# Bias-table copies in DRAM: the outermost dimension of the copies changed from the pair of heads (4) to query column and head (32)

## The chip, the cores and the metric

The kernel runs on one core of one Trainium2 chip. The metric is device time in microseconds (us). Three runs before the change took 1340.88, 1342.46 and 1348.09 us; the median is 1342.46 us.

## The reference, cut to what matters

One encoder layer over 2048 tokens of width 1024: an input projection, then two branches side by side (neighbourhood attention of 8 heads on a 32 x 64 grid, and a bidirectional mLSTM of 4 heads), an output projection, a gated residual and a last RMSNorm. What the change touches is the additive bias of the attention:

```python
dy = row_idx - r[:, None] + NA_KH - 1
dx = jnp.clip(col[None, :] - col[:, None], -(NA_KW - 1), NA_KW - 1) + NA_KW - 1
bias = rpb[:, dy[:, None, :, None], dx[None, :, None, :]]
s = jnp.einsum('bhrcd,bhrjkd->bhrcjk', qg, kg).astype(jnp.float32) + bias[None]
s = jnp.where(col_mask[:, None, :], s, -jnp.inf)
```

`rpb` has 8 heads x 15 row offsets x 31 column offsets. The kernel works on patches of 8 x 16 queries, and for each kind of patch (3 kinds of rows x 3 kinds of columns) it needs a table with the negated bias of every query against every key of the patch's window, and 1e30 where the window does not reach.

The layer's other work that the change lies beside: a centred convolution of width 5 with a SiLU over the mLSTM's q and k, the transposes of k, and the output weight multiplied by the gate.

## The kernel before, in words

**Stages.** (1) `start` normalises the tokens and computes the first two v/o blocks of the projection. (2) `tok_blocks` computes blocks 2 to 5, with tokens on partitions: v and o of two mLSTM heads (tiles `pvo`, stored through `stvo`) and the attention's v (tiles `pv`, stored through `stv`), 128x256 matmuls, 16 tiles a block. Beside them run the mLSTM's decay tables: `decays` loads a row of `d_mneg` into one of six tiles `dec` (line 822, on the SP queue), GpSimd masks it (826), ScalarE takes four exponentials (833), and the ACT queue stores it to `d_ck` (835); 32 such tiles. (3) `conv_blocks` computes blocks 6 to 9 with channels on partitions: 32 tiles `pc` of 24 matmuls of 128x512 each (lines 546 to 548). ScalarE evicts each into a tile `u` (line 891, 4 buffers), VectorE makes the convolution `acc` of five operations (926 and 928, 5 buffers), ScalarE applies SiLU (930), SP stores it (933). For k, TensorE then transposes it (`kt`, line 939, four transposes), ScalarE copies that into one of two stage tiles `stk` (941), and SP stores it (943). In the same stage `gated_out` loads the output weight in 16 halves `wraw` (854, two buffers), VectorE multiplies each by the gate (861), SP stores it to `d_wo` (862). (4) `phase1b` and `phase2` do the mLSTM, the rest of the projection (tiles `pq`, line 986) and the attention; the tables are loaded there into `tab` (1450).

**The bias tables.** They are made in DRAM alone, by copies on the SP queue. `tables_begin` writes the negated `rpb` to `d_rneg` and fills the column tables `d_e` with 1e30; `tables_columns` then copies for each of the 16 query columns of a kind the 16 column offsets that it sees: 3 kinds x 16 = 48 copies `d_e<-d_rneg` of 4 x 30 x 16 floats (line 648). `tables_rows` copies for each kind of columns, kind of rows and query row 8 rows of the column table into `d_t`: 3 x 3 x 8 = 72 copies `d_t<-d_e` (line 670) of 4 x 32 pieces, each of 8 x 24 or 8 x 32 floats (768 or 1024 bytes). In both, the outermost 4 is the pair of heads, and the next dimension is the query column and the head of the pair (2), or the head of the pair and the row offset.

**Order of the work.** Stages (2) and (3) are ordered by a scheduler that places each engine's instructions by its own estimate of their costs, DMAs included. Each queue then runs strictly in that order: an instruction that waits holds up all that stand behind it on its engine. The scheduler also gives the DMAs of the SP and ACT queues eight completion semaphores in turn, so that a DMA waits, before its issue, for the landing of the one that used its semaphore last. The stage (4) is ordered by hand.

Of the kernel before, what the change touches and what calls it, by code (L numbers as in the profile page):

```python
# [62 lines left out]
class Kernel:  # L63
# [576 lines left out]
    def tables_columns(self, ct):  # L640
        nc = self.nc
        c0 = (0, 16, 48)[ct]
        k0 = (0, 8, 40)[ct]
        for i in range(16):
            c = c0 + i
            start = min(max(c - 8, 0), GRID_W - 16)
            dx = start - c + 15
            nc.sync.dma_start(self.d_e[ct][:, i, :, :, start - k0 : start - k0 + 16].rearrange("h e a k -> h (e a) k"), self.d_rneg.rearrange("(h e) a k -> h (e a) k", e=2)[:, :, dx : dx + 16])

    def table_fills(self):  # L650
        nc = self.nc
# [8 lines left out]
    def tables_rows(self, ct, rt):  # L660
        nc = self.nc
        nk = (24, 32, 24)[ct]
        pr = (0, 1, 3)[rt]
        t = self.d_t[rt][ct]
        for r in range(8):
            row = 8 * pr + r
            start = min(max(row - 4, 0), ROWS - 8)
            dy = start - row + 7
            j0 = (start - PR_R0[pr]) * nk
            nc.sync.dma_start(  # L670
                t[:, r * 16 : (r + 1) * 16, :, j0 : j0 + 8 * nk].rearrange("h q e n -> h (q e) n"),
                self.d_e[ct][:, :, :, dy : dy + 8, :].rearrange("h c e a k -> h (c e) (a k)"),
            )


# [1140 lines left out]
```

## Time and profile before

| what | value |
|---|---|
| three runs, us | 1340.88, 1342.46, 1348.09 |
| the profiled execution, us | 1339.01 |
| its span, us (1.81 us lie around it) | 1337.2 |
| mean granted TensorE clock | 0.992 |
| TensorE matmul busy | 1296.3 us, 97% |
| VectorE busy | 780.4 us, 58% |
| ScalarE busy | 541.6 us, 41% |
| GpSimd busy | 224.6 us, 17% |
| DMA | 255.89 MB, 228645 packets, mean 191 GB/s |
| `d_t<-d_e` on SP, line 670 | 72 issues, 281.6 to 484.2 us |
| `d_e<-d_rneg` on SP, line 648 | 48 issues, 143.2 to 280.5 us |

In a row of the profile, PE is TensorE's matmul, PEld its weight load, DVE VectorE, ACT ScalarE, POOL GpSimd and SPq the SP queue, which issues DMAs. Times are us from the span's start unless a row says ns; three numbers with slashes are the least, the median and the greatest of a group, in ns. PEclk is the share of full clock that TensorE was granted. The DMA share is the mean over the core's 16 DMA engines of the time in which they had packets; packets that wait in an engine's queue can take it over 1. Matmuls overlap in TensorE, so that a busy share of 97% is no measure of what is left; the idle time and the clock are.

### The profile page before, as it was taken

To read this page: it belongs to the slowest core of one execution; us is meant where nothing else is said; L and a number is where in the kernel's file an instruction comes from. 1 tells how busy PE (TensorE), PEld (TensorE's weight loads), DVE (VectorE), ACT (ScalarE), POOL (GpSimd) and SP (SyncE) were. 2 spreads that over 40 slices of the span, in tenths; PEclk is the share of its full clock that TensorE was granted. 3 is DMA by queue.
4 is the path that set the end of the run, shared out by engine and by line. 5 is a ranking of instruction groups with operands and counts; after the bars stand their busy time and mean duration, and the time that the engine had idled before them with its cause. 6 is when DMAs were issued, how large, how long until landed. Compare 5 with 4: busy or idle time off the path is not lost.

```text
span 1337.2 us, 23272 instructions
## 1 busy us (share of the span) xinstructions
PE 1296.3 (97%) x8330; PEld 1116.4 (83%) x8330; DVE 780.4 (58%) x2406; ACT 541.6 (41%) x1184; POOL 224.6 (17%) x278
## 2 busy tenths in 40 slices
PE   9999999999999879999999999999998999999996
PEld 8899999999888667888888888888776777778785
DVE  5645442112552929456677877777647676766663
ACT  5653325542212403223333423333346555565551
POOL 0243103441000000001212102212102211212211
PEclk9999999999999999999999999999999999999999
DMA  9997547896364856644665867755678876767771
GB/s 324 331 268 186 160 136 185 220 232 182 107 160 125 199 139 187 194 119 138 190 181 177 248 200 207 224 174 172 199 251 234 217 206 184 193 179 192 201 185 48
DMA packets 228645, 255.89 MB, mean 191 GB/s; under 512 B 29734, under 2 KB 177958, under 8 KB 228530
## 3 DMA queue, kind: packets, MB, share of 16 engines
q1 hardware_dynamic: 145326, 182.97, 48.2%
q0 software_dynamic: 20464, 36.21, 10.9%
q10 hardware_dynamic: 62740, 35.22, 9.1%
q8 instruction: 66, 1.08, 0.3%
q14 instruction: 49, 0.40, 0.1%
HBM read 169.81 MB, written 92.72 MB: 196 GB/s over the span
## 4 chain that ended last, share of the span: by engine, by line
PE 64%; DMA 14%; issue 7%; DVE 6%; SPq 5%; ACT 2%; POOL 1%; ACTq 0%; POOLq 0%; DVEq 0%
PE pq L986 20%; PE y L1566 12%; SPq L670 4%; PE pvo L546 3%; PE pO L1521 3%; PE pvo L548 3%; PE pvo L547 3%; PE pvo L601 3%; PE pT L1506 3%; DMA d_ck<-dec 3%; PE pS L1478 2%; DMA tab<-d_t 2%; DMA dec<-d_mneg 2%; PE pi L1227 2%; PE px L1225 2%
## 5 line engine op out<-in xcount | busy, mean ns | idle before, releaser
L986 PE MATMUL pq<-hhi,whi_a 128*128 128x512 f32 x512 | 208.4, 407 | 2.0 <-ACT u L891 2.0
L986 PE MATMUL pq<-hlo,whi_a 128*128 128x512 f32 x512 | 208.1, 406 | 0.0
L986 PE MATMUL pq<-hhi,wlo_a 128*128 128x512 f32 x512 | 206.7, 404 | 0.0
L986 PEld LDWEIGHTS pq<-hhi,whi_a 128*128 128x128 f32 x512 | 96.8, 189 | 18.7 <-ACT u L891 2.5
L986 PEld LDWEIGHTS pq<-hhi,wlo_a 128*128 128x128 f32 x512 | 96.8, 189 | 16.6
L986 PEld LDWEIGHTS pq<-hlo,whi_a 128*128 128x128 f32 x512 | 96.8, 189 | 16.1 <-issue 0.5
L1508 ACT ACTIVATE pt<-pT 96x384 f32<-96x384 f32 (+3 forms) x128 | 65.7, 514 | 84.0 <-PE pT L1506 81.1
L960 POOL TENSOR_TENSOR wlo_a<-rawq,whi_a 128x1024 fp32r<-128x1024 f32 x19 | 45.8, 2411 | 316.2 <-ACT whi_a L959 282.0
L1487 ACT ACTIVATE pbuf<-pbuf,mn 128x480 f32<-128x480 f32 (+5 forms) x128 | 76.0, 595 | 50.7 <-DVE mn L1486 50.6
L1566 PE MATMUL y<-hhi,whi_a 128*128 128x512 f32 x256 | 90.7, 416 | 0.5 <-ACT whi_a L1536 0.5
L1566 PE MATMUL y<-hhi,wlo_a 128*128 128x512 f32 (+1 forms) x272 | 90.6, 399 | 0.2 <-ACT y L1573 0.2
L1230 ACT ACTIVATE num<-px,gtile 128x129 f32<-128x129 f32 x120 | 38.2, 365 | 112.8 <-PE px L1225 90.7
L1486 DVE CUSTOM_DVE_ANT_0 pbuf<-pS,tab 128x480 f32<-128x480 f32 (+5 forms) x128 | 62.4, 539 | 36.7 <-PE pS L1478 29.0
L618 DVE TENSOR_TENSOR stvo<-pvo,brow 128x256 f32<-128x256 f32 x64 | 26.6, 423 | 83.7 <-PE pvo L548 64.6
L1506 PEld LDWEIGHTS pT<-ident,pbuf 128*128 128x128 f32 (+2 forms) x416 | 50.6, 136 | 27.0 <-issue 6.9
L546 PE MATMUL pvo<-whi_b,hhi 128*128 128x256 f32 x256 | 72.6, 284 | 0.0
L1506 PE MATMUL pT<-ident,pbuf 128*128 128x128 f32 (+2 forms) x416 | 66.8, 273 | 5.9 <-DVE pbuf L1498 4.3
L548 PE MATMUL pvo<-whi_b,hlo 128*128 128x256 f32 x256 | 72.0, 281 | 0.0
L547 PE MATMUL pvo<-wlo_b,hhi 128*128 128x256 f32 x256 | 72.0, 281 | 0.0
L1249 POOL TENSOR_TENSOR hm<-hm,ck 128x128 f32<-128x128 f32 x64 | 26.4, 412 | 253.0 <-DVE hm L1248 223.1
L833 ACT ACTIVATE dec<-dec,gtile 128x128 f32<-128x128 f32 x128 | 42.2, 392 | 48.8 <-POOL dec L826 42.7
L546 PE MATMUL pc<-hhi,whi_b 128*128 128x512 f32 x128 | 51.6, 403 | 7.6 <-ACT u L891 7.6
(302 smaller groups left out, 3374.7 us busy)
## 6 DMA issues: line engine op xcount, KB each, us to landing
ck<-d_ck SPq DMA_DIRECT2D x64, 384.5 KB
rawq<-in_w_main_dram SPq DMA_DIRECT2D x28, 512.0 KB
raw<-in_w_main_dram SPq DMA_DIRECT2D x20, 512.0 KB
d_ck<-stvo SPq DMA_DIRECT2D x16, 514.0 KB
kv<-d_ck SPq DMA_DIRECT2D x64, 128.5 KB
wada<-in_w_ada_dram SPq DMA_DIRECT2D x32, 256.0 KB
dec<-d_mneg SPq DMA_DIRECT2D x32, 256.0 KB
d_ck<-dec ACTq DMA_DIRECT2D x32, 256.0 KB
```

The source lines that it names most:

```text
L546: nc.tensor.matmul(ps, lhi(k), rhi(k), start=(k == 0), stop=False)
L547: nc.tensor.matmul(ps, lhi(k), rlo(k), start=False, stop=False)
L548: self.mark = nc.tensor.matmul(ps, llo(k), rhi(k), start=False, stop=(k == KT - 1))
L670: nc.sync.dma_start(t[:, r * 16 : (r + 1) * 16, :, j0 : j0 + 8 * nk].rearrange("h q e n -> h (q e) n"), self.d_e[ct][:, :, :, dy : dy + 8, ...
L833: nc.scalar.activation(t[:, o, :], t[:, o, :], AF.Exp, bias=self.cols["g"][:, d, h, c : c + 1])
L960: (eng or nc.gpsimd).tensor_tensor(lo[:, :, cs], raw, hi[:, :, cs].bitcast(F32), ALU.subtract)
L986: self.mark = nc.tensor.matmul(patch_ps(ps) if patch else ps, w, self.htok(h, g, k, patch), start=(k == 0 and n == 0), stop=(k == KT - 1 a ...
L1486: nc.vector.tensor_tensor_reduce(pt[:, :nk], ps, tabs[place[u]][:, j * nk : (j + 1) * nk], 1.0, 3e38, ALU.add, ALU.min, mn)
L1487: nc.scalar.activation(pt[:, :nk], pt[:, :nk], AF.Exp, bias=mn, scale=-1.0, accum_out=sums[:, j : j + 1])
L1506: nc.tensor.transpose(ps[:cs, i, :], U[u][j][:, i * cs : (i + 1) * cs], self.ident)
L1508: nc.scalar.activation(t[:cs, :nch, :], ps[:cs, :nch, :], AF.Copy)
L1566: nc.tensor.matmul(y, m[:, k, :], w[k][:, cs], start=(k == 4 and n == 0), stop=(k == 3 and n == 2))
```

## The change

The two calls name the same source and target elements, in another order of dimensions. The sizes of the contiguous pieces, the number of copies and the tables are the same; the outermost dimension is 30 (head of the pair and row offset) instead of 4 in line 648, and 32 (query column and head of the pair) instead of 4 in line 670.

```diff
-            nc.sync.dma_start(self.d_e[ct][:, i, :, :, start - k0 : start - k0 + 16].rearrange("h e a k -> h (e a) k"), self.d_rneg.rearrange("(h e) a k -> h (e a) k", e=2)[:, :, dx : dx + 16])
+            nc.sync.dma_start(self.d_e[ct][:, i, :, :, start - k0 : start - k0 + 16].rearrange("h e a k -> (e a) h k"), self.d_rneg.rearrange("(h e) a k -> (e a) h k", e=2)[:, :, dx : dx + 16])
...
-                t[:, r * 16 : (r + 1) * 16, :, j0 : j0 + 8 * nk].rearrange("h q e n -> h (q e) n"),
-                self.d_e[ct][:, :, :, dy : dy + 8, :].rearrange("h c e a k -> h (c e) (a k)"),
+                t[:, r * 16 : (r + 1) * 16, :, j0 : j0 + 8 * nk].rearrange("h q e n -> (q e) h n"),
+                self.d_e[ct][:, :, :, dy : dy + 8, :].rearrange("h c e a k -> (c e) h (a k)"),
```

The scheduler's order of the stages (2) and (3) changes with it, on SP, VectorE, ScalarE and TensorE; GpSimd's stays.

The SP queue in the middle of stage (3). The rows with - are how it stood, those with + what stands there now; `d_t_76`, `d_t_79` and `d_t_82` are tables of the second kind of columns, `raw_0_4320` and `raw_1_4322` the weights of block 8, `acc_k`, `stk` and `wraw` as above:

```order
-L933 DMA d_ck<-acc_k_1_4262 128x4x128
-L854 DMA wraw_4268<-in_w_out_dram 128x512
-L862 DMA d_wo<-wraw_4172 128x512
-L207 DMA raw_0_4320<-in_w_main_dram 128x1024
-L207 DMA raw_1_4322<-in_w_main_dram 128x1024
-L670 DMA d_t_76<-d_e_73 4x32x256 x8
-L670 DMA d_t_79<-d_e_73 4x32x256 x8
-L670 DMA d_t_82<-d_e_73 4x32x256 x8
+L207 DMA raw_1_4730<-in_w_main_dram 128x1024
+L854 DMA wraw_5052<-in_w_out_dram 128x512
+L862 DMA d_wo<-wraw_4972 128x512
+L933 DMA d_ck<-acc_k_2_4312 128x4x128
```

A batch of 24 table copies stood between two stores of the convolution. It has left this place, as have the batch of 24 of the third kind of columns further on and the 19 copies that stood last before the first `gate` load. Of the 72 copies, 7 are left in stage (3), one to three at a time, all within its first part.

The SP queue late in stage (2), among the loads of the decay tiles; `stv_2_3153` is the third of the four stores of block 4, `raw_1_3449` the second half of block 6's weights:

```order
-L648 DMA d_e_74<-d_rneg 4x30x16
-L670 DMA d_t_75<-d_e_72 4x32x192
 L822 DMA dec_3289<-d_mneg 128x512
+L586 DMA d_vna<-stv_2_3153 128x4x256
+L207 DMA raw_1_3449<-in_w_main_dram 128x1024
 L822 DMA dec_3326<-d_mneg 128x512
+L670 DMA d_t_79<-d_e_73 32x4x256
 L822 DMA dec_3360<-d_mneg 128x512
-L586 DMA d_vna<-stv_2_3153 128x4x256
 L822 DMA dec_3395<-d_mneg 128x512
```

The copies `d_t<-d_e` now stand here, 32 of them between the first and the last load of a decay tile, where 23 of the small copies `d_e<-d_rneg` and 2 of `d_t<-d_e` stood; the 48 small copies stand earlier, in runs of up to nine. Twenty-two more copies `d_t<-d_e` stand between the last decay tile and the first load of stage (3). The store of `stv_2_3153` has moved two decay tiles up, and the one behind it (`stv_3_3293`) as well.

VectorE early in stage (3), at the second tile of the convolution:

```order
 L928 SCALAR_TENSOR_TENSOR acc_k_1_4072<-u_0_1_4029,cw,acc_k_1_4072 128x512
+L861 TENSOR_TENSOR wraw_4078<-wraw_4078,gate 128x512
+L861 TENSOR_TENSOR wraw_4172<-wraw_4172,gate 128x512
 L898 MEMSET u_0_3_4105 128x2
 L896 COPY u_0_1_4029<-u_0_2_4066 128x2
```

The 16 products of output weight and gate were spread over stage (3) up to its end; now all of them stand among the first eleven of its 32 tiles. On TensorE the transposes `kt` of a tile stand right ahead of the fourth tile after it throughout; before, they stood there for the first five tiles only, and up to nine tiles behind for the others.

## Prediction

> **What bounds the kernel now.** I read the page first, then the windows of stage (3), the waits there, and what the SP queue did at those times.
>
> ```profile
> PE 1296.3 (97%) x8330; PEld 1116.4 (83%) x8330; DVE 780.4 (58%) x2406; ACT 541.6 (41%) x1184; POOL 224.6 (17%) x278
> ```
>
> TensorE sets the time: only 40.9 us of the span (1337.2 − 1296.3) are without a matmul. A change to DMAs alone can win no more than its share of these, and what the clock loses. The windows show a good part of both in the stage that the large table copies touch.
>
> ```profile
> 329.10:375.70 46.60, 46.60 (x213) 37.97 (x212) 20.07 (x44) 11.71 (x17) 0.00 (x0) 1.00 0.32 92
> ...
> 440.00:460.00 20.00, 15.61 (x69) 11.85 (x69) 17.76 (x39) 9.54 (x16) 0.00 (x0) 0.91 1.08 248
> ...
> 480.00:500.00 20.00, 13.65 (x59) 10.74 (x57) 5.07 (x9) 0.66 (x2) 0.00 (x0) 0.95 0.67 161
> 500.00:520.00 20.00, 18.71 (x74) 15.15 (x75) 19.04 (x42) 8.68 (x13) 0.00 (x0) 0.88 0.82 220
> 520.00:533.10 13.10, 11.05 (x49) 8.63 (x47) 13.10 (x25) 5.04 (x8) 1.19 (x1) 1.00 0.50 141
> 333.00:350.00 17.00, 17.00 (x75) 13.76 (x75) 8.63 (x20) 4.70 (x6) 0.00 (x0) 1.00 0.28 80
> ...
> 459.00:484.00 25.00, 25.00 (x112) 20.38 (x111) 9.35 (x21) 6.14 (x8) 0.00 (x0) 1.00 0.31 94
> ```
>
> Each row is a stretch with its length, the busy time of PE, PEld, DVE, ACT and POOL, the granted clock and the DMA share. In the first row PE is busy without a gap: eight of the 32 `pc` tiles, at full clock. In four later stretches it stands idle for 20 − 15.61 = 4.39, 20 − 13.65 = 6.35, 20 − 18.71 = 1.29 and 13.10 − 11.05 = 2.05 us, 14.1 us in all, and in three of them the clock is 0.91, 0.95 and 0.88, which costs (busy time by the share missing) 1.4 + 0.7 + 2.2 = 4.3 us more. Stretches without idle time have a clock of 1.00.
>
> What PE waited for, from 338 to 540 us (time, count, longest):
>
> ```profile
> ACT stk L941 <- DMA d_ck<-stk: 48.7, 8, 20.3
> ...
> DVE acc_q L926 <- DMA d_ck<-acc_k: 22.6, 2, 22.1
> DVE acc_k L926 <- DMA d_ck<-acc_k: 18.9, 3, 17.7
> ...
> PE pc L546 <- ACT u L891: 7.6, 1, 7.6
> ...
> PE kt L939 <- ACT acc_k L930: 4.3, 3, 2.1
> ```
>
> PE waited for ScalarE's evictions (`u`) and activations (`acc_k`); ScalarE and VectorE in turn stood up to 20.3 and 22.1 us behind stores `d_ck<-stk` and `d_ck<-acc_k`. The SP queue shows why these were late:
>
> ```profile
> 330.20 20.53 SPq L670 DMA_DIRECT2D d_t<-d_e  x19
> ...
> 377.16 0.94 SPq L862 DMA_DIRECT2D d_wo<-wraw  x2
> ...
> 379.30 1.37 SPq L854 DMA_DIRECT2D wraw<-in_w_out_dram  x2
> ...
> 392.62 33.43 SPq L670 DMA_DIRECT2D d_t<-d_e  x24
> ...
> 427.57 1.24 SPq L933 DMA_DIRECT2D d_ck<-acc_k  x1
> ...
> 455.67 29.70 SPq L670 DMA_DIRECT2D d_t<-d_e  x24
> ```
>
> Three batches of table copies hold SP for 20.53, 33.43 and 29.70 us; PE works through them from its buffers and stops after each of the last two: the `d_ck<-acc_k` at 427.57 is among the first stores behind the second batch.
>
> **What a copy costs.**
>
> ```profile
> L670 SPq DMA_DIRECT2D d_t<-d_e x72: 562/1166/2413, 281.6 to 484.2; - x72
> ```
>
> ```profile
> L648 SPq DMA_DIRECT2D d_e<-d_rneg x48: 561/572/975, 143.2 to 280.5; - x48
> ```
>
> An issue takes 0.56 us where nothing holds it, and 29.70 / 24 = 1.24 us in a batch. In the batches (333 to 350 and 459 to 484 us above) the DMA share is 0.28 and 0.31, near 4 of 16 engines: the copies ran on as many engines as their outermost dimension is long. A copy has 128 pieces, so each of four engines took 1.24 us for 32 of them, and the fourfold batch rate says that the engines, not SP, were full. With 32 outermost, the 16 engines have 8 pieces each: 1.24 / 4 = 0.31 us, under the 0.56 us of the issue. So a copy costs SP between 0.56 (the least in the rows) and 1.24 us (nothing changes); I take 0.56, since the share in the rows speaks for the engine count as cause. The Trainium skill, "DMA: Bandwidth & Descriptors", section "Why a DMA increments its semaphore by 16 and not by 1", has the rule: the engines used are the largest number up to 16 that divides the slowest dimension of both sides, so 4 before, 16 and (for 30) 15 after. By that rule 0.56 is the only value; the shares of 0.28 and 0.31 agree with its 4.
>
> **What moves out of stage (3).** By the order, 65 of the 72 large copies leave it, and the 7 left, one to three at a time, cost SP 7 × 0.56 = 4 us, hidden as long as a store may be 1.7 us late (below: 7 us of room). The three batches' 20.53 + 33.43 + 29.70 = 83.7 us of SP time go; the conv stores no longer stand behind them.
>
> What PE could win there at most follows from its pace:
>
> ```profile
> L546 PE MATMUL pc<-hhi,whi_a x128: 387/397/628, 329.1 to 476.1; 128*128 128x512 f32 x128
> ...
> L546 PE MATMUL pc<-hhi,whi_b x128: 390/393/796, 375.7 to 530.2; 128*128 128x512 f32 x128
> ```
>
> ```profile
> 351.52 0.44 PE kt L939 x4
> ```
>
> ```profile
> 530.63 0.40 PE L548 MATMUL pc<-hhi,wlo_b 128*128 128x512 f32 x1
> ...
> 533.08 0.50 PE L986 MATMUL pq<-hhi,whi_a 128*128 128x512 f32 x1 [2.05 <-ACT u L891]
> ```
>
> The first block takes 375.7 − 329.1 = 46.60 us with five of the 16 groups of transposes (0.44 us each, 2.2 us), so 44.4 us without. Three more with the other 11 groups take 133.2 + 4.8 = 138.0 us: the stage could end at 513.7 us, and `pq` start some 1.0 us later (an eviction of 0.7 us, 11.71 / 17 in the first window, and the hand-over, my estimate), at 514.7. It started at 533.08. So at most 18.4 us are to be had, and idle time plus clock above say the same: 14.1 + 4.3 = 18.4.
>
> **What is late next there: the output weight.** All 16 products `wraw` by `gate` now stand among the first eleven tiles, in order on VectorE between convolutions. Two buffers serve them, and a buffer's round is a product, a store, and a load behind it.
>
> ```profile
> L861 DVE TENSOR_TENSOR wraw<-wraw,gate x16: 678/683/693, 376.4 to 540.0; 128x512 f32<-128x512 f32 x16
> ```
>
> ```profile
> 427.57 7.87 DMA d_ck<-acc_k
> ...
> 439.81 4.63 DMA d_wo<-wraw
> ...
> 444.50 4.61 DMA wraw<-in_w_out_dram
> ...
> 498.89 3.12 DMA d_wo<-wraw
> ...
> 502.08 6.27 DMA wraw<-in_w_out_dram
> ```
>
> In the chain of waits a round is 4.63 + 4.61 + 0.68 = 9.9 us between 439 and 449 us, where the DMA share is 1.08, and 3.12 + 6.27 + 0.68 = 10.1 us later. In the quiet part the next pair's load is issued at 379.30, 2.14 us after the store at 377.16: 2.1 + 4.6 + 0.7 = 7.4 us. The order wants eight pairs in ten tiles of 46.60 / 8 = 5.83 us, 58.3 / 8 = 7.3 us a pair. VectorE, held by a late product, is then behind by 8 × (7.4 − 7.3) = 1 to 8 × (9.9 − 7.3) = 21 us. PE notices only beyond its room: a tile's convolution needs the next tile's eviction; after that come 0.7 us of eviction, 20.07 / 8 = 2.5 of VectorE and 0.7 of SiLU, with the hand-overs some 4.1 us; the transposes come two tiles (11.7 us) after that tile's end. The room is 11.7 − 4.1 = 7.6 us, so PE loses 0 to 13 us. Of the copies only seven are beside it, so I take a round in the middle (8.7 us), 11 us behind and 3 us lost. Stage (3): −18.4 + 3 = **−15.4 us**.
>
> **What moves into stage (2).** Thirty-two large copies stand among the 32 loads of decay tiles, in place of 23 small and 2 large ones, and 22 more behind the last. PE is busy there throughout, and what could stop it is one chain:
>
> ```profile
> 216.62 5.28 DMA dec<-d_mneg
> ...
> 224.79 8.14 DMA d_ck<-dec
> ...
> 298.29 7.36 DMA d_vna<-stv
> 305.77 0.44 DVE stv L581
> 306.25 0.39 PE pv L546
> ```
>
> ```profile
> DVE stv L581 <- DMA d_vna<-stv: 24.9, 5, 11.1
> ...
> PE pv L546 <- DVE stv L581: 0.7, 1, 0.7
> ```
>
> ```profile
> L822 SPq DMA_DIRECT2D dec<-d_mneg x32: 319/350/1188, 200.6 to 303.9; - x32
> ```
>
> The stores of `stv` stand among the loads of decay tiles on SP, and a load waits for the store of the tile six before it. Already VectorE waits up to 11.1 us for them, and PE 0.7 us: no slack at the end of the chain. But the stores `stv_2_3153` and `stv_3_3293` stand two decay tiles earlier now, and a tile takes (303.9 − 200.6) / 31 = 3.3 us: 6.7 us of new slack. Against it stand the copies. SP has 32 copies there in place of 25: 7 × 0.56 = 4 us more of issues, spread over 103 us, where a decay tile needs one load of 0.35 us every 3.3 us: nothing on the path. The engines pay 0.31 us in each load and, at most, in each store: 0.6 us a round, and the chain passes 32 / 6 = 5.3 rounds, so 3.3 us, within the 6.7. I cost it at nothing; without that cover it would be 3.3 us. The 22 copies behind the last load take 22 × 0.56 = 12 us and were 19 in 20.53 us before. The small copies, 30 outermost in place of 4, cost the same 0.56 us and only stand earlier.
>
> After 533 us the order is by hand and PE is 97% busy over the span; I take the rest as shifting whole.
>
> **Sum.** The profiled execution took 1339.01 us: 1339.01 − 15.4 = 1323.6. The median of the runs is 3.45 us above it; 1342.46 − 15.4 = 1327.1, **1327.0 us**.
>
> **The rivals.** *The output weight takes most of it back.* If each round keeps to the rows' 9.9 us, PE loses up to 13 us, which leaves 18.4 − 13 = 5.4, and 3 if half of the clock's 4.3 us goes too; with half of both lost it wins 11: 1331 to 1339. For it: both dense rows of the trace; against it: in those rows the engines were full or the stores had piled up behind the copies.
>
> *The copies get no cheaper.* If an issue still takes 1.24 us, the 7 left in stage (3) cost 8.7 us in place of 4, and 32 × 1.24 = 40 us of SP lie among the decay loads. The order alone still takes the batches away; each round of the decay chain is longer by 1.24 − 0.31 = 0.93 us, 0.93 × 5.3 = 5 us at its end: 15.4 − 5 = 10 us, some 1332. Against it: the shares of 0.28 and 0.31.
>
> *Slower, by stage (2).* The copies now lie on every engine that the decay tiles and `stv` use. The store at 427.57, right behind 24 copies, took 7.87 us, where `d_wo` took 3.12 later. If a round of the decay chain grows by that 4.75 us, its end slips by 5.3 × 4.75 = 25 us, of which 6.7 are covered by the earlier stores only if these don't wait as well; PE waits the 25, and with 15.4 won the kernel is 10 us slower, 1352. It decides from (6.7 + 15.4) / 5.3 = 4.2 us a round. From 1.6 to 4.2 us a round the kernel is unchanged. For it: no slack in the chain, and VectorE's 24.9 us of waiting. Against it: a copy keeps an engine for 0.31 us, and one stands ahead of a load, not 24. The Trainium skill, same page, section "Issuing engines are not separate DMA queues", says that all DMAs interleave on the same 16 engines whoever starts them, so that spreading the copies cannot shield the others; the 7.87 us agrees.
>
> **How the numbers follow.** A measurement of this kernel tells 0.5%, 6.7 us, from no change. Forecast, the gain of 10 to 18 us: 0.66. The output weight: 0.13, half of it beyond 6.7 us of gain. Copies no cheaper: 0.07. The chain of stage (2), no change: 0.05; slower: 0.09. Faster 0.66 + 0.065 + 0.07 = 0.79, same 0.065 + 0.05 = 0.12, slower 0.09. The range reaches from a little over the whole of the gain, 1342.46 − 18.4 = 1324 less 4 for runs as far below the median as the profiled one, 1320, to 1341, which takes in the first two rivals and leaves out the chain.
>
> **What would show it.** Right: no copies of 1.24 us in a row between 375 and 485 us; `d_t<-d_e` at a median near 0.56 us; the waits of DVE and ACT for `d_ck` stores in stage (3) under 5 us; the first `pq` 12 to 18 us earlier against the first `pc`, with the clock near 1.00. Wrong: PE waiting for `pv` or the first `pc` later than 329.1 us (the decay chain); PE waiting for `kt` with VectorE behind `wraw` (the output weight); `d_t<-d_e` still at 1.2 us (copies no cheaper); or a gain in stage (3) given back after the first `pq`.

## The result, and the profile after

The changed kernel takes 1335.73 us in the median of 13 runs (1332.29 to 1339.78), the kernel before 1343.35 us (1340.37 to 1349.49): a ratio of 0.9945, 95% interval 0.993 to 0.9961. It is 7.6 us faster, half of the 15.4 us forecast. The change did what it says, and stage (3) gave more than the sum had; stage (2), which was costed at nothing, took 11 us back.

Where the time went is read from three marks: the first matmul of block 4 (`pv`), of stage (3) (`pc`) and of stage (4) (`pq`). The rows of the changed kernel that carry them, and the windows of two short stretches of stage (2) and of the whole stage (3) (columns as in the prediction; the last but two is the granted clock):

```profile
L546 PE MATMUL pv<-whi_a,hhi x128: 276/280/283, 242.3 to 287.3; 128*128 128x256 f32 x128
```

```profile
L546 PE MATMUL pc<-hhi,whi_a x128: 388/393/481, 340.1 to 480.1; 128*128 128x512 f32 x128
```

```profile
L986 PE MATMUL pq<-hhi,whi_a x512: 387/394/502, 526.5 to 1004.8; 128*128 128x512 f32 x171
```

```profile
187.00:190.40 3.40, 3.40 (x18) 3.40 (x19) 1.78 (x4) 0.00 (x0) 0.00 (x0) 0.53 0.26 60
...
314.80:320.20 5.40, 5.40 (x25) 5.40 (x26) 2.81 (x4) 2.56 (x8) 2.57 (x2) 0.50 0.80 202
```

```profile
340.10:526.50 186.40, 185.56 (x835) 150.50 (x833) 122.17 (x242) 58.87 (x86) 2.41 (x1) 1.00 0.50 143
```

Each trace was taken twice:

| us | before | before, again | changed | changed, again |
|---|---|---|---|---|
| first `pv` | 237.2 | 236.8 | 242.3 | 244.2 |
| first `pv` to first `pc` | 91.9 | 92.2 | 97.8 | 95.8 |
| first `pc` to first `pq` | 204.0 | 203.3 | 186.4 | 186.5 |
| first `pq` to the end | 804.1 | 806.4 | 807.1 | 804.6 |
| span | 1337.2 | 1338.7 | 1333.6 | 1331.1 |

Stage (3) is 17 to 18 us shorter, with 0.84 us of idle time in 186.40 and a clock of 1.00. Two losses lie ahead of it: 5 to 7 us before the first `pv`, and 4 to 6 between it and the first `pc`; together 11.0 us in both pairs of traces. What lies behind the first `pq` differs between two traces of the same kernel by as much as between the two kernels, so I read no effect in it.

The waits of PE in the changed kernel up to the first `pq` name the two places (total, count, longest):

```profile
PE pv L546 <- DVE stv L581: 4.1, 1, 4.1
PE ps_c_w L713 <- DVE gtile L803: 3.4, 1, 3.4
PE pq L986 <- ACT u L891: 0.8, 1, 0.8
```

The first in time is `ps_c_w`, a transpose of the decay tables' preparation (line 713). The chain of waits of the changed kernel leads to it from the SP queue:

```profile
175.97 0.78 SPq L648
...
176.79 0.78 SPq L648
...
179.71 6.29 DMA d_ck<-stvo
...
186.13 0.43 DVE stvo L618
186.56 0.21 DVE gtile L803
...
186.90 0.30 PE ps_c_w L713
```

In order: SP issues small copies one behind the other, only then the store `d_ck<-stvo`; VectorE waits for its landing to have the stage tile back, and the small operation `gtile`, for which PE waits, stands behind that on VectorE. SP's own timeline shows how long the line was:

```profile
156.15 7.82 SPq L648 DMA_DIRECT2D d_e<-d_rneg  x9
164.08 0.97 SPq L504 DMA_DIRECT2D ga<-in_w_ada_dram  x2
165.15 0.38 SPq L626 DMA_DIRECT2D d_ck<-stvo  x1
165.58 5.09 SPq L648 DMA_DIRECT2D d_e<-d_rneg  x6
170.77 0.97 SPq L504 DMA_DIRECT2D ga<-in_w_ada_dram  x2
171.79 6.75 SPq L648 DMA_DIRECT2D d_e<-d_rneg  x8
178.64 0.97 SPq L504 DMA_DIRECT2D ga<-in_w_ada_dram  x2
179.71 0.38 SPq L626 DMA_DIRECT2D d_ck<-stvo  x1
```

The loads `ga` (line 504, rows of the weight from which the gate is made) stand in the same line, and VectorE waits for them as well:

```profile
182.27 1.41 DVE L515 SCALAR_TENSOR_TENSOR gsum<-ga,cact,gsum 128x512 f32<-128x512 f32 x2 [4.12 <-DMA ga<-in_w_ada_dram]
```

The store, landed at 179.71 + 6.29 = 186.00 us, is the later of the two and so sets the end of the wait.

The second loss comes down the decay chain, as in the trace of before, but with more at its end:

```profile
302.18 3.99 DMA dec<-d_mneg
...
306.23 7.88 DMA d_vna<-stv
...
314.23 0.44 DVE stv L581
...
314.71 0.58 PE pv L546
```

Each of the two waits costs more than its own length, since the matmuls behind it come slower (start, length; the wait in brackets):

```profile
183.09 0.28 PE L547 MATMUL pvo<-wlo_a,hhi 128*128 128x256 f32 x1
183.21 0.28 PE L548 MATMUL pvo<-whi_a,hlo 128*128 128x256 f32 x1
186.90 0.30 PE L713 MATMUL ps_c_w<-ident,wide 128*128 128x128 f32 x1 [3.41 <-DVE gtile L803]
...
189.65 0.41 PE L547 MATMUL pvo<-wlo_a,hhi 128*128 128x256 f32 x1
189.87 0.41 PE L548 MATMUL pvo<-whi_a,hlo 128*128 128x256 f32 x1
```

Ahead of the wait one starts every 0.12 us, behind it every 0.21 to 0.22, and the granted clock is 0.53 from 187.0 to 190.4 us and 0.50 from 314.8 to 320.2 us, behind the second wait. So 3.4 us of waiting came to 5.1 us at the first `pv`. The 4.1 us of the second came to 6.8 at the first `pc`, counted from the 91.0 us of the runs below without a wait there; that is 5.9 more than before, where PE waited 0.7 us. The Trainium skill, "TensorE: Matmul & The Clock Gate", section "Part 1: The HAM clock gate (the "warmup" mystery)", has the clock fall to half after an idle window of about 3.4 us; the granted clock of 0.53 and 0.50 behind waits of 3.4 and 4.1 us agrees.

The copies themselves:

```profile
L670 SPq DMA_DIRECT2D d_t<-d_e x72: 528/595/1638, 197.4 to 368.1; - x72
```

```profile
L648 SPq DMA_DIRECT2D d_e<-d_rneg x48: 779/780/1257, 142.5 to 195.6; - x48
```

A large copy costs SP 0.53 to 0.60 us in place of 1.17. A small one costs 0.78 us in place of 0.57, and all 48 are issued by 196 us, where they had been spread to 280.

### The profile page after: what moved, and what is told of

Read it like the earlier page. It is cut to its first block, busy times and chain, and to the rows that moved or that the text cites. A ratio compares the mean times of both kernels' runs of the same rounds, so it can differ in the third digit from the quotient of the medians.

```text
span 1333.6 us, 23276 instructions
## 1 busy us (share of the span) xinstructions
PE 1298.3 (97%) x8330; PEld 1119.2 (84%) x8330; DVE 781.4 (59%) x2406; ACT 542.6 (41%) x1184; POOL 224.7 (17%) x278
## 4 chain that ended last, share of the span: by engine, by line
PE 71%; DMA 14%; DVE 6%; issue 3%; ACT 2%; SPq 1%; POOL 1%; ACTq 0%; POOLq 0%; DVEq 0%
PE pq L986 19%; PE y L1566 12%; PE pc L547 4%; PE pc L548 4%; PE pc L546 4%; PE pT L1506 3%; PE pO L1521 3%; PE pvo L601 3%; DMA dec<-d_mneg 3%; PE pS L1478 2%; DMA d_ck<-stvo 2%; PE pvo L546 2%; PE pvo L547 2%; PE pvo L548 2%; DMA tab<-d_t 2%
## 5 line engine op out<-in xcount | busy, mean ns | idle before, releaser
L986 PEld LDWEIGHTS pq<-hhi,whi_a 128*128 128x128 f32 x512 | 96.8, 189 | 17.8 <-ACT u L891 1.3
L833 ACT ACTIVATE dec<-dec,gtile 128x128 f32<-128x128 f32 x128 | 42.0, 392 | 55.5 <-POOL dec L826 53.3
L581 DVE TENSOR_TENSOR stv<-pv,brow 128x256 f32<-128x256 f32 x32 | 12.7, 422 | 79.7 <-DMA d_vna<-stv 43.3
```

Of the source, the lines that this page charges most:

```text
L833: nc.scalar.activation(t[:, o, :], t[:, o, :], AF.Exp, bias=self.cols["g"][:, d, h, c : c + 1])
L986: self.mark = nc.tensor.matmul(patch_ps(ps) if patch else ps, w, self.htok(h, g, k, patch), start=(k == 0 and n == 0), stop=(k == KT - 1 a ...
```

## The experiments

Theory A: the small copies, dearer and standing ahead of the stores of `stvo`, make the first loss; the large copies among the decay loads make the second; the win of stage (3) comes from the large copies being cheap there, or gone. Theory B: order alone makes the win, and the load on all 16 engines the losses. Each ratio is to the kernel before, with its 95% interval. The marks come from the same rows as above, in each kernel's own trace.

| kernel | median us | ratio | first `pv` | to first `pc` | to first `pq` |
|---|---|---|---|---|---|
| changed | 1335.73 | 0.9945 (0.993 to 0.9961) | 242.3 | 97.8 | 186.4 |
| c_only | 1345.52 | 1.0041 (1.0021 to 1.0061) | 242.4 | 91.3 | 203.5 |
| t_only | 1322.83 | 0.9852 (0.9814 to 0.989) | 237.6 | 92.3 | 186.4 |
| rows_late | 1326.31 | 0.9885 (0.9845 to 0.9925) | 242.1 | 91.0 | 186.4 |
| cols_late | 1337.2 | 0.9968 (0.9948 to 0.9988) | 238.5 | 103.9 | 186.4 |
| dummies | 1328.52 | 0.9906 (0.9874 to 0.9939) | 242.4 | 91.0 | 186.4 |
| rows_pool | 1332.03 | 0.9932 (0.991 to 0.9954) | 245.5 | 91.0 | 186.4 |
| spread4 | 1335.82 | 0.9969 (0.9939 to 0.9998) | 239.5 | 97.5 | 186.4 |
| t_rows_late | 1321.47 | 0.9859 (0.9839 to 0.9879) | 236.9 | 91.0 | 186.5 |

**One part of the change alone: c_only, the small copies.**

```diff
 # against the kernel before
-... "h e a k -> h (e a) k"), ... "(h e) a k -> h (e a) k", ...
+... "h e a k -> (e a) h k"), ... "(h e) a k -> (e a) h k", ...    # line 648
```

> Only the 48 small copies d_e<-d_rneg have their new outermost dimension (30); the 72 large ones stay as before. On SP the small copies then stand as in the changed kernel, in runs of up to nine ahead of the stores of stvo, and the three batches of large copies stand in stage (3) as before. Theory A (small copies cost 0.78 us each and hold up the stores of stvo; large copies among the decay loads cost the second loss; the win of stage (3) is the large copies' cheapness): ps_c_w waits about 3.4 us and the first pv comes at about 242.3 us (before 237.2); no wait of pv over 1 us later, since few copies stand among the decay loads; first pc to first pq about 204 us as before. In all some 4 to 5 us slower than before, about 1347. Theory B (the losses come from the large copies' traffic on all 16 engines alone): first pv at 237 and the time of before, 1343.

Its trace has the first loss in full, and the large copies at their old price in the old batches:

```profile
L648 SPq DMA_DIRECT2D d_e<-d_rneg x48: 779/780/1513, 142.4 to 195.8; - x48
```

```profile
PE ps_c_w L713 <- DVE gtile L803: 3.7, 1, 3.7
```

First `pv` at 242.4, and no wait of `pv` behind it; stage (3) took 203.5 us as before. This half of the change alone makes the kernel 4.9 us slower (1345.52 against 1340.66 on that chip), as A said; B's "as before" falls.

**The other part alone: t_only, the large copies.**

```diff
 # against the kernel before, lines 671 and 672
-... "h q e n -> h (q e) n"), ... "h c e a k -> h (c e) (a k)"),
+... "h q e n -> (q e) h n"), ... "h c e a k -> (c e) h (a k)"),
```

> Only the 72 large copies d_t<-d_e have their new outermost dimension (32); the small ones stay as before. 41 of the large ones then stand in stage (3), one to four at a time, 18 behind the last decay load and 13 among the last decay loads. Theory A: no wait of ps_c_w, first pv at 237; the wait of pv on stv at most 2 us; first pc to first pq about 187 to 190 us, since copies of 0.56 us a few at a time hold nothing: 15 to 17 us faster than before, about 1327. Theory B (stage (3) gains only because the copies have left it): with 41 of them back in it, first pc to first pq 195 us or more and a gain of under 10 us, about 1335.

```profile
L986 PE MATMUL pq<-hhi,whi_a x512: 387/394/496, 516.3 to 992.5; 128*128 128x512 f32 x171
```

```profile
L670 SPq DMA_DIRECT2D d_t<-d_e x72: 528/597/947, 284.1 to 428.8; - x72
```

```profile
PE pv L546 <- DVE stv L581: 0.6, 2, 0.5
```

1322.83 us: 17.8 us faster than before. The 41 large copies that stand in stage (3) again, at 0.53 to 0.60 us and a few at a time, cost it nothing: 186.4 us, to the tenth what the changed kernel has with seven of them (both counted by the order on SP). So the copies need not leave the stage for the win, and theory B falls here too. The lower price and the spreading of the copies that came with it are enough together. How much each does was not tried, and no kernel was run in which copies at the old price leave the stage.

**The large copies behind the decay loads: rows_late.** An order alone, drawn when the program is built.

```diff
 # against the changed kernel
-            self.behind(nc.sync.dma_start(t, src.broadcast_to([P, 512])), self.mark)
+            self.last_dec = nc.sync.dma_start(t, src.broadcast_to([P, 512]))
+            self.behind(self.last_dec, self.mark)
...
+            self.behind(copy, self.last_dec)      # each copy of tables_rows
```

> The changed kernel, with the large copies ordered behind the last load of a decay tile (an order alone, no wait is added). The small copies stand as in the changed kernel. Theory A: the first loss stays (ps_c_w waits about 3.4 us, first pv at 242.3), the second goes (pv waits under 1 us, first pc about 334 in place of 340.1), stage (3) about 188 us: some 5 us faster than the changed kernel, about 1330. If the large copies among the decay loads are not the cause of the second loss: first pc stays at about 340 and the time at 1336.

First `pv` at 242.1 with `ps_c_w` waiting 3.6 us: the first loss stayed. The second went: no wait of `pv`, 91.0 us to the first `pc`. It was 4 us better than expected, 1326.31.

**The small copies behind block 2: cols_late.**

```diff
 # against the changed kernel
+            if n == 0:
+                self.block2 = self.mark
...
+            self.behind(copy, self.block2)        # each copy of tables_columns
```

> The changed kernel, with the small copies ordered behind the last matmul of block 2 (an order alone). They then stand among the first half of the decay loads, and the large ones among the second half and in stage (3). Theory A: the first loss goes (no wait of ps_c_w, first pv at 237), the second stays or grows, since as many copies lie among the decay loads, of 0.78 us in place of 0.53 (pv waits 4 us or more); stage (3) about 188 us: some 4 us faster than the changed kernel or equal to it, 1331 to 1336. If the first loss has nothing to do with where the small copies stand: first pv stays at 242.

The first loss fell from 5.1 to 1.3 us, with the copies at the same 0.78 us, so their place matters. The second grew, with most of the small copies among the decay loads too. Two of its four waits, 4.2 us together, are for stores of `stvo`, the other two for stores of `stv`, so a part of it is the first loss in a later place:

```profile
PE pv L546 <- DVE stv L581: 9.5, 4, 4.1
```

The first `pc` came at 342.4. Upper end of what was expected and a little past it, 1337.2.

**Place or price? spread4.** Small copies in their old form, written into block 2 so that they stand where the changed kernel has them.

```diff
 # against t_only
+            if h == 2:
+                for _ in range(3):
+                    next(self.columns, None)      # one copy of tables_columns each
...
-            if n > 0:
-                self.tables_columns(n - 1)
```

> The kernel t_only (small copies 4 outermost as before, large ones 32), with the small copies written into block 2, three behind each of its tiles, so that they stand on SP where the changed kernel has them (48 between 142 and 200 us, in runs of up to six), at the old 0.57 us each in place of 0.78. It tells whether their place or their price makes the first loss. If the place alone does it: first pv at 241 to 242 us and ps_c_w waits 3 us, as in the changed kernel. If the price is needed (48 x 0.21 = 10 us more of SP's time): first pv at 238 or earlier. The large copies then stand among the decay loads again: a wait of pv of 0 to 3 us; first pc to first pq 186.4. Time 1323 to 1330.

First `pv` at 239.5, between the two, 1.9 us behind t_only's 237.6: `ps_c_w` did not wait, but two waits of `pvo` came to 2.0 us. The longer of them, 1.2 us at 216.6, stood behind an addition to the gate's row on VectorE (`grow`, line 526), 20 us after the last small copy, so that not all of the 1.9 need be due to their place. Of the 5.1 us the place alone makes 1.9 at most, and the dearer issue the rest; the places are alike, not the same, so the split is rough. The large copies are among the decay loads again here, and PE loses time there again (`pv` waits 4.5 us), but in another way: 4.3 us of it stand behind a split of weights on VectorE, for which ScalarE's half came late, right behind exponentials of the decay tiles that had been held up:

```profile
276.81 1.23 DVE L212 TENSOR_TENSOR wlo_b<-raw,whi_b 128x1024 fp32r<-128x1024 f32 x1 [13.34 <-ACT whi_b L211]
```

Its runs spread from 1331.58 to 1344.91, more than those of the other new kernels; the marks, from one trace, are the firmer evidence.

**How the large copies slow the decay chain: dummies and rows_pool.**

```diff
 # dummies, against rows_late
+            self.behind(nc.sync.dma_start(self.d_x[n], self.d_rneg[0, 0:2]), self.last_dec)
```

```diff
 # rows_pool, against the changed kernel, line 670
-            nc.sync.dma_start(
+            nc.gpsimd.dma_start(
```

> The kernel rows_late with one tiny copy (2 x 31 floats, into a scratch of its own) right behind each of the 32 loads of decay tiles on SP; the large copies stay behind the last load. It tells how the large copies slow the decay chain. Theory Q (by their place in the queue: each takes one of the eight completion semaphores in turn and stands ahead of the next load): the second loss comes back without their traffic: the 32 loads take 105 us or more (rows_late 93, the changed kernel 110), pv waits 2 us or more, first pc at 336 or later (rows_late 333.1), the time 1329 to 1333. Theory E (by their bytes on the 16 engines): loads in 95 us, no wait of pv, first pc at 333, time as rows_late, 1326.

> The changed kernel with the 72 large copies issued by GpSimd in place of SP: the same bytes in the same stretch, 33 of them or more among the decay tiles, but no place in SP's queue. The small copies stay on SP. Theory Q (place in SP's queue): the first loss stays (ps_c_w waits 3.5 us, first pv at 242), the second goes: first pc at 333 to 335, the time 1326 to 1329. Theory E (bytes on the engines): the second loss stays, first pc at 338 or later, time 1333 or more. GpSimd's own issues (0.55 us each where the trace of before shows them, line 1450) may delay the masks by as much a tile.

Neither theory held whole. In the kernel before and in the changed one, PE's wait ends with the landing of the fourth store of block 4 (`stv_4_3`, line 586). The rows of that store on SP, of rows_late, dummies and rows_pool in turn; it stands behind 29 of the 32 decay loads in all three, as in the changed kernel:

```profile
295.40 0.38 SPq L586 DMA_DIRECT2D d_vna<-stv  x1
```

```profile
299.77 0.38 SPq L587 DMA_DIRECT2D d_vna<-stv  x1
```

```profile
306.48 0.38 SPq L586 DMA_DIRECT2D d_vna<-stv  x1
```

Counted from each one's first `pv`, that is 53.3, 57.4 and 61.0 us; the changed kernel has 306.23 − 242.3 = 63.9. One tiny copy behind each load costs 4.1 us, with hardly any bytes; the bytes without a place in SP's line, with GpSimd's issues ahead of the masks, cost 7.7; the changed kernel has 10.6 more. Of these, 4.3 lie ahead of the first decay load: it comes 34.6 us ahead of the first `pv` in the changed kernel, where eleven large copies stand before it, and 38.9 in the three others. Nor does a place in the line always cost: t_rows_late (below) has 23 of the old small copies among its loads, and its store comes 91.9 us after its first load, that of rows_late 92.2.

When the store comes and what `pv` waits for, in all traces:

| kernel | fourth store behind first `pv`, us | `pv` waits, us | of it for this store |
|---|---|---|---|
| rows_late | 53.3 | 0 | |
| t_rows_late | 55.2 | 0 | |
| dummies | 57.4 | 0 | |
| before, again | 60.3 | 1.0 | all |
| rows_pool | 61.0 | 0 | |
| before | 61.1 | 0.7 | all |
| c_only | 61.9 | 0 | |
| t_only | 62.1 | 0.6 | 0.2 |
| changed, again | 62.6 | 3.3 | all |
| changed | 63.9 | 4.1 | all |
| spread4 | 65.9 | 4.5 | none |
| cols_late | 74.5 | 9.5 | 1.2 |

So there is no sharp bound in the time of issue. Up to 57.4 us PE never waits; from 60 to 62 some kernels wait a little and others do not, as the landing differs too: it took 7.36 us before, to 68.4 us behind the first `pv`, and 5.92 in c_only, to 67.8. In t_only, spread4 and cols_late PE waits, in whole or in the main, for other stores or for the split of weights.

Still, dummies' store came early enough, and its time hardly moved (1328.52 against 1326.31, the intervals overlap) though its loads took 103.5 us in place of rows_late's 98.8 (not 93, as the expectation has it). In rows_pool the second loss is gone and the first is larger (`ps_c_w` waits 4.8 us, first `pv` at 245.5), which was not expected. Its trace shows GpSimd issuing the first 25 large copies from 162.4 to 194 us, beside SP's small ones, where the changed kernel starts them at 197.4; that may be why, and no run isolates it.

**before_again and after_again**, for second traces:

> The kernel before, unchanged, for a second trace. If its executions differ in one place, the marks show where: first pc at 329.1, first pq at 533.1 and 804.1 us behind it in the first trace. Theory: the first two repeat within 1 us, what lies behind first pq varies by some us.

> The changed kernel, unchanged, for a second trace. Theory: ps_c_w waits 3.4 us and pv 4 us again, first pc at 340 and first pq at 526.5 within 1.5 us; what lies behind first pq (807.1 us in the first trace) varies by some us.

Stage (3) repeats within 0.7 us and the first `pc` within 0.1; the first `pv` of the changed kernel moved by 1.9, and what lies behind the first `pq` by 2.3 and 2.5.

**The version that beats both: t_rows_late**, t_only with the order of rows_late.

> The kernel t_only with its large copies ordered behind the last load of a decay tile, as in rows_late: neither loss is left. First pv at 237.5, first pc 91.0 us later at 328.5 (t_only 329.9), first pq 186.4 later at 515: 1 us faster than t_only, 1320 to 1324, which the measurement cannot tell from t_only's 1322.8.

1321.47 us, no wait of PE from 130 us to the end of stage (2), 91.0 us to the first `pc`. From t_only's 1322.83 it cannot be told, as expected; both beat the kernel before by 18 to 19 us and, by the ratios, the change as made by about 12 (0.9945 − 0.9852 = 0.0093, and 0.0086).

## Why the prediction was right and wrong, step by step

*What bounds the kernel; what a large copy costs.* Right: 0.53 to 0.60 us in place of 1.17, as the step took it (0.56). That holds for a few at a time: seven or eight in a row took SP 4.8 and 8.8 us in t_rows_late, 0.7 to 1.1 us each.

*What moves out of stage (3).* The size was right: at most 18.4 us, and 17.6 were won (16.8 in the second pair). The reason had a gap: the step counted on 65 copies leaving, and t_only shows that cheap ones need not. The rival in which copies get no cheaper loses its ground with the price.

*What is late next: the output weight.* The mechanism was there and cost nothing. VectorE waited for `wraw` eleven times, and the last product came late:

```profile
DVE wraw L861 <- DMA wraw<-in_w_out_dram: 17.1, 11, 3.5
```

```profile
L861 DVE TENSOR_TENSOR wraw<-wraw,gate x16: 682/692/694, 348.6 to 410.3; 128x512 f32<-128x512 f32 x16
```

Ten tiles from 340.1 end at 398.4, so the last product was 12 us behind, close to the 11 taken; but no `kt` waited. The 3 us charged for it, from a room of 7.6 us, were too much. How much room there is was not tried.

*The small copies "cost the same 0.56 us and only stand earlier".* This step failed, in both halves. They cost 0.78, and what they were moved past, the stores of `stvo` and the loads `ga`, was not looked at. Measured: 5.1 us at the first `pv` (7.4 in the second pair); c_only shows that these copies alone do it.

*"I cost it at nothing": the decay chain.* This failed too, by its size. The step had 3.3 us of lengthening against 6.7 of new slack. Between before and after, the store `stv_4_3` came 63.9 − 61.1 = 2.8 us later behind the first `pv` although it stands two loads earlier: 6.7 + 2.8 = 9.5 us of lengthening, of which 36.6 − 34.6 = 2.0 lie ahead of the first decay load, and the room was already used up. The step took the issues on SP for "nothing on the path", counted a copy's share of engine time alone, and only for copies among the loads; in dummies 32 copies of almost no bytes made the store 4.1 us later. How the 9.5 us divide between place and bytes stays open. The rival "slower, by stage (2)" had the right place: 9.5 us over 5.3 rounds are 1.8 us a round, near the lower end of the 1.6 to 4.2 that it gave for "unchanged" and far from the 4.2 from which it would have decided.

*The sum.* −17.6 in stage (3), +5.1 and +5.9 in stage (2), +3.0 behind the first `pq` (scatter): −3.6 us of span in the first pair of traces; −16.8 + 7.4 + 3.6 − 1.8 = −7.6 in the second, which is also what the medians say. The forecast's −15.4 lacked the 11 us of stage (2); with the 3 us charged to the output weight taken out, it would have been −18.4 + 11 = −7.4. That 1335.73 lies between the 1320 and 1341 of the prediction is luck: this range was drawn for the output weight and for copies that get no cheaper, neither of which happened, and left out the chain of stage (2), which did.

## What to carry to other kernels

When a scheduler places by its own estimate of costs, a change to the form of a transfer can move it in the order; here the small copies moved ahead of others although each had become dearer. List for each queue what the moved transfers now stand in front of, and price that, before counting what they freed. Cost every line of a diff by itself and try the parts alone: here one of two like-looking edits was worth 18 us and the other cost 5. A chain that already makes the bound engine wait a little has no cover, and small additions count on it; a pause of 3.3 us or more brought slow matmuls behind it on top here.

## What the runs showed of the hardware that was not expected

- A copy with a longer outermost dimension is not always cheaper to issue: 4 x 30 x 16 floats took SP 0.56 us at the least and 30 x 4 x 16, the same 120 pieces, 0.78, while 4 x 32 and 32 x 4 pieces of 768 or 1024 bytes took 0.56 and 0.53. Why was not tried.
- Waits of TensorE of 1.5 and 2.7 us in cols_late left the granted clock behind them at 1.00; waits of 3.3 to 4.8 us, in eight of the twelve traces, brought it to between 0.50 and 0.65. After the 3.4 us in the changed kernel a 128x256 matmul started every 0.21 us in place of 0.12, still so 3 us later. Two windows of cols_late, behind the waits of 2.7 and 4.1 us:

```profile
265.90:270.00 4.10, 4.10 (x35) 4.10 (x36) 2.02 (x4) 3.00 (x8) 2.23 (x2) 1.00 0.94 215
...
304.40:309.00 4.60, 4.60 (x22) 4.60 (x23) 0.84 (x3) 0.00 (x0) 0.95 (x1) 0.50 0.94 242
```

- Two traces of one kernel differed by up to 2.5 us behind the first `pq`, in a part whose program the change hardly touches; marks inside the span tell more than the span.
